# A hybrid attention/mLSTM block: q/k of three mLSTM heads and the branch gates by seven half-size products

## The chip, the cores and the metric

One Trainium2 chip, one core of it. The metric is the device time of one execution in microseconds. The kernel before takes 1360.22 us (median of 3 runs, 1359.88 to 1360.26).

## The reference

One layer on x of 512 tokens and width 1024, float32:

```python
f = swiglu(rmsnorm(x, ffn1_pre_g), w_gate, w_up, w_down)         # d_ff = 2816
x = x + 0.5 * rmsnorm(f, ffn1_post_g)
h = rmsnorm(x, mix_pre_g)
P = h @ w_in        # attention q,k,v | mLSTM q,k | mLSTM v,o | mLSTM i,f | branch gates g_a,g_m
A = dilated_window_attention(...)                  # 4 head slots of 128, 3 groups combined
qk = silu(causal_depthwise_conv(qk_m))             # width 4
M = sigmoid(o) * headnorm(mlstm(q_m, k_m, v_m, i, f))            # 4 heads of 256
y = (sigmoid(g_a) * (A @ w_att) + sigmoid(g_m) * (M @ w_mlstm)) @ w_out
x = x + rmsnorm(y, mix_post_g)
x = x + 0.5 * rmsnorm(swiglu(rmsnorm(x, ffn2_pre_g), ...), ffn2_post_g)
```

## The kernel before

Activations stand transposed in SBUF: `hTh` and `hTl` hold the high and the low part of h (128 partitions, 8 blocks of the width, 512 tokens), and every product with a weight is three matmuls for each of 8 blocks: weight high with h high, weight high with h low, weight low with h high. `load_w` (line 78) brings one weight of 128 x 1024 by a DMA on SyncE's queue into `wf` (3 buffers), casts it on ACT into `wh` and subtracts on DVE into `wl` (5 buffers each; the trace names a buffer after one of its users). `ws` (line 168) does the 24 matmuls of 128 x 512 into one PSUM bank; there are 8 banks.

The stages run one after the other: FFN a (to about 366 us), the attention (to 624), the four mLSTM heads (to 834), the merge (to 965), `w_out` (to 1011), FFN b. Both FFNs make 18 of their units by a form with seven half-size products in place of eight: the operands are cut into quarters (256 tokens, half of the width), sums of quarters of h are made once (`parts`), sums of quarters of the weights for each unit on DVE, and the unit is 7 products of 12 matmuls of 128 x 256 (`seven`, line 278, `product` at line 319). There the order of all engines is written by hand, and DVE's adds read a bank while PE is in the other one.

In the mixer the order on each engine is set by a scheduler when the kernel is built; it can move an instruction of one part between those of another, but each engine then runs its list strictly in order. For a head h: `m_vo(h)` (v and output gate, 96 matmuls), `m_scores`, then the pair of products `m_qk_proj(h + 1, 0)` with its conv `m_qk_conv` (line 874: ACT makes `z`, six DVE ops add the shifted terms, ACT `th`, DVE `z`, ACT cast `mqkh`, DVE `mqkl`), `m_out(h)` (`po`), the pair and conv for `pi` = 1, `m_decay(h + 1)` (`pb`) and `m_turn(h)` (`pml`). The conv reads the pair's two PSUM banks. For the last head the two pairs are those of gates 0 and 1 (`branch_gates`, line 1091). In the merge, for each of 8 `dt`, come 12 matmuls of attention with `wA`, 24 of mLSTM with `wM`, the combination on DVE and ACT, and then the gates' pair of `dt` + 2. The attention's output is kept in SBUF as `atth`, `attl` (lines 861 and 862), and the residual x in four tiles through the whole kernel. The gains of the norms and the small constants come in by POOL's queue, which also computes the norms' powers (`r_pf`, `r_mx`, `r_m`).

Of the kernel before, what the change touches and what calls it, by code (L numbers as in the profile page):

```python
# [39 lines left out]
def tile_hybrid_block(ctx: ExitStack, tc: tile.TileContext, a: dict):  # L40
# [1050 lines left out]
    def branch_gates(dt):
        wg = [load_w(a["wgm"][dt, b], f"gm{dt}{b}") for b in range(2)]
        p1 = pair(f"p1_{dt}")
        for b in range(2):
            ws(p1[b], wg[b], KD, hTh, hTl)
        t1 = work.tile([P, 2, T], F32, tag=("h", "tmp")[dt % 2], bufs=1, name=f"t1_{dt}")
        for b in range(2):
            nc.scalar.activation(t1[:, b, :], p1[b], AF.Tanh, scale=0.5)
# [35 lines left out]
    for dt in range(KD):
        if dt % 2 == 0:
            wA = load_w(a["wA"][dt // 2], f"wA{dt}")
        wM = load_w(a["wM"][dt], f"wM{dt}")
# [2 lines left out]
        ws(p2[0], (wA[0][:, o:o + 512], wA[1][:, o:o + 512]), HEADS, atth, attl)  # L1140
        ws(p2[1], wM, KD, mlTh, mlTl)
        t1 = t1s[dt]
        for b in range(2):
            nc.vector.scalar_tensor_tensor(t1[:, b, :], t1[:, b, :], 1.0, p2[b], op0=ALU.add, op1=ALU.mult)  # L1144
        nc.vector.tensor_tensor(t1[:, 0, :], t1[:, 0, :], t1[:, 1, :], op=ALU.add)
        nc.scalar.mul(meTh[:, dt, :], t1[:, 0, :], 0.5)
        nc.vector.scalar_tensor_tensor(meTl[:, dt, :], t1[:, 0, :], 0.5, meTh[:, dt, :].bitcast(F32),
                                       op0=ALU.mult, op1=ALU.subtract)
# [123 lines left out]
```

## Time and profile before

| | us |
|---|---|
| median of 3 runs | 1360.22 |
| the profiled execution | 1361.59 |
| its span, first to last instruction | 1359.8 |
| PE busy | 1344.6 (99%) |
| PE weight loads (PEld) | 1202.8 (88%) |
| DVE busy | 968.4 (71%) |
| ACT busy | 601.7 (44%) |
| POOL busy | 30.1 (2%) |

The profiled execution is a single one, with 1361.59 us of its own; its span is what the hardware profiler shows from the first instruction to the last. Busy time is the union of an engine's instructions. A matmul's row lasts longer than the distance to the next one, because matmuls are pipelined: the distance from start to start is what one costs. The same holds in a smaller way for DVE and ACT, where an instruction begins a little before the one ahead has ended.

### The profile page before, as it was taken

The numbers are of one execution on the slowest core, as the hardware profiler recorded it, in microseconds if no ns is written. First come the engines' busy times: TensorE is split into PE (matmuls) and PEld (weight loads), VectorE is DVE, ScalarE is ACT, GpSimd is POOL, SyncE is SP. The second block draws the span as 40 slices with busy tenths as digits, with TensorE's granted clock in tenths as the row PEclk, the third lists the DMA queues.
The fourth block names the chain that finished last, engine by engine and source line by source line (L and its number), as shares of the span: only waits on it lengthen the run. The fifth ranks groups of instructions, "written<-read, shape, count | busy, mean of one in ns | idle before, by whom it ended". The sixth has DMA issues, their size and how long they took to land.

```text
span 1359.8 us, 19896 instructions
## 1 busy us (share of the span) xinstructions
PE 1344.6 (99%) x7976; PEld 1202.8 (88%) x7976; DVE 968.4 (71%) x1482; ACT 601.7 (44%) x969; POOL 30.1 (2%) x52
## 2 busy tenths in 40 slices
PE   8999999999999999999999999999999999999998
PEld 7899999878899889888888888888889999998786
DVE  7789898896772885675756754333378798997983
ACT  5444444555633532435545443222264444444552
POOL 1000000000200000000000000000010000000000
PEclk8999999999999999999999999999999999999999
DMA  5333333654233222222222232233213233335541
GB/s 201 94 109 95 109 109 109 232 171 150 69 93 123 78 78 91 81 78 78 78 78 78 78 108 79 95 107 100 95 47 116 94 94 108 109 104 194 174 150 62
DMA packets 40829, 145.91 MB, mean 107 GB/s; under 512 B 4652, under 2 KB 4652, under 8 KB 40736
## 3 DMA queue, kind: packets, MB, share of 16 engines
q1 hardware_dynamic: 39600, 141.08, 31.7%
q0 software_dynamic: 1136, 3.56, 0.8%
q8 instruction: 62, 1.02, 0.3%
q14 instruction: 31, 0.25, 0.1%
HBM read 142.53 MB, written 2.10 MB: 106 GB/s over the span
## 4 chain that ended last, share of the span: by engine, by line
PE 89%; DVE 6%; ACT 2%; issue 2%; DMA 1%; SPq 0%; DVEq 0%; POOLq 0%; ACTq 0%
PE p L176 11%; PE qb_b L319 9%; PE qb_a L319 9%; PE pq L176 8%; PE pm L176 6%; PE qa_b L319 4%; PE qa_a L319 4%; PE acc_o L227 3%; PE pvo L991 2%; PE pvo L993 2%; PE pvo L992 2%; PE pg_a L186 2%; PE pq L186 2%; PE pg_b L186 2%; PE pg_a L176 2%; PE pg_b L176 2%
## 5 line engine op out<-in xcount | busy, mean ns | idle before, releaser
L176 PE MATMUL pq<-hTh_mx,wh_qk 128*128 128x512 f32 x160 | 63.2, 395 | 0.0
L176 PE MATMUL pq<-hTl_mx,wh_qk 128*128 128x512 f32 x160 | 62.4, 390 | 0.0
L88 DVE TENSOR_TENSOR wl_qk<-wf_qk,wh_qk 128x1024 fp32r<-128x1024 f32 x24 | 29.3, 1221 | 41.6 <-ACT wh_qk L86 31.3
L176 PE MATMUL pm<-hTh_mx,wh_mqk 128*128 128x512 f32 x128 | 50.3, 393 | 0.0
L991 PE MATMUL pvo<-wh_vo,hTh_mx 128*128 128x512 f32 x128 | 50.2, 392 | 0.0
L176 PE MATMUL pm<-hTl_mx,wh_mqk 128*128 128x512 f32 x128 | 49.9, 390 | 0.0
L176 PE MATMUL p<-hTh_mx,wh_gm 128*128 128x512 f32 x128 | 49.9, 390 | 0.0
L993 PE MATMUL pvo<-wl_vo,hTh_mx 128*128 128x512 f32 x128 | 49.8, 389 | 0.0
L176 PE MATMUL p<-hTl_mx,wh_gm 128*128 128x512 f32 x128 | 49.8, 389 | 0.0
L992 PE MATMUL pvo<-wh_vo,hTl_mx 128*128 128x512 f32 x128 | 49.8, 389 | 0.0
L86 ACT CAST wh_qk<-wf_qk 128x1024 fp32r<-128x1024 f32 x24 | 25.0, 1045 | 56.1 <-PE pw L739 28.8
L1144 DVE SCALAR_TENSOR_TENSOR t<-t,p 128x512 f32<-128x512 f32 x16 | 11.0, 688 | 42.7 <-PE p L176 42.7
L88 DVE TENSOR_TENSOR wl_mqk<-wf_mqk,wh_mqk 128x1024 fp32r<-128x1024 f32 x16 | 19.6, 1223 | 29.7 <-ACT wh_mqk L86 25.3
L176 PE MATMUL pq<-hTh_mx,wl_qk 128*128 128x512 f32 x160 | 39.6, 389 | 0.0
L882 DVE SCALAR_TENSOR_TENSOR z<-pm,cw,z 128x511 f32<-128x511 f32 (+2 forms) x48 | 35.3, 743 | 1.4 <-ACT z L880 0.9
L319 PE MATMUL qa_a<-hTl_f,wh_a 128*128 128x256 f32 x144 | 36.1, 283 | 0.0
L319 PE MATMUL qa_b<-hTl_f,wh_b 128*128 128x256 f32 x144 | 36.1, 283 | 0.0
L319 PE MATMUL qa_a<-hTh_f,wh_a 128*128 128x256 f32 x144 | 36.1, 283 | 0.0
L319 PE MATMUL qa_b<-hTh_f,wh_b 128*128 128x256 f32 x144 | 36.1, 283 | 0.0
L247 ACT CAST wh_a<-cd_a 128x1024 fp32r<-128x1024 f32 x18 | 18.9, 1050 | 38.9 <-DVE cd_a L247 38.9
L247 ACT CAST wh_b<-cd_b 128x1024 fp32r<-128x1024 f32 x18 | 18.9, 1050 | 37.8 <-DVE cd_b L247 37.8
L176 PEld LDWEIGHTS pq<-hTh_mx,wl_qk 128*128 128x128 f32 x160 | 30.0, 188 | 6.2
(677 smaller groups left out, 4421.1 us busy)
## 6 DMA issues: line engine op xcount, KB each, us to landing
wf_qk<-in_wqk SPq DMA_DIRECT2D x24, 512.0 KB, 3.7
B_a<-in_wdq SPq DMA_DIRECT2D x21, 512.0 KB, 4.1
B_b<-in_wdq SPq DMA_DIRECT2D x21, 512.0 KB, 3.9
g_a<-in_wgu SPq DMA_DIRECT2D x18, 512.0 KB, 3.8
u_a<-in_wgu SPq DMA_DIRECT2D x18, 512.0 KB, 3.8
g_b<-in_wgu SPq DMA_DIRECT2D x18, 512.0 KB, 3.8
u_b<-in_wgu SPq DMA_DIRECT2D x18, 512.0 KB, 3.7
wf_mqk<-in_wmqk SPq DMA_DIRECT2D x16, 512.0 KB, 3.3
```

What stands on the lines that cost most here:

```text
L86: nc.scalar.copy(wh, wf)
L88: nc.vector.tensor_tensor(wl, wf, wh.bitcast(F32), op=ALU.subtract)
L176: nc.tensor.matmul(out, lhsT=wt[:, k * P:(k + 1) * P], rhs=x[:, k, tok], start=n == 0, stop=n == len(terms) - 1)
L186: nc.tensor.matmul(outs[b][:, tok], lhsT=ws_[b][w][:, k * P:(k + 1) * P], rhs=x[:, k, tok], start=i + k + hf == 0, stop=hf == 1 and i == 2 ...
L227: nc.tensor.matmul(out, lhsT=x[:, tk], rhs=w[:, cs], start=first and n == 0, stop=last and n == 2, skip_group_check=True)
L247: self.last[eng] = getattr(getattr(nc, eng), fn)(*args, **kw).ins
L319: nc.tensor.matmul(out, lhsT=wt[:, i * P:(i + 1) * P], rhs=y[:, i, :], start=first and n == 0, stop=last and n == len(terms) - 1, skip_gro ...
L882: nc.vector.scalar_tensor_tensor(z[:, s:], src[:, :T - s], cw[:, ct, 3 - s:4 - s], z[:, s:], op0=ALU.mult, op1=ALU.add)
L991: nc.tensor.matmul(out, lhsT=hTh[:, k, tk], rhs=wh[:, cs], start=k == 0, stop=False)
L992: nc.tensor.matmul(out, lhsT=hTl[:, k, tk], rhs=wh[:, cs], start=False, stop=False)
L993: nc.tensor.matmul(out, lhsT=hTh[:, k, tk], rhs=wl[:, cs], start=False, stop=k == KD - 1)
L1144: nc.vector.scalar_tensor_tensor(t1[:, b, :], t1[:, b, :], 1.0, p2[b], op0=ALU.add, op1=ALU.mult)
```

## The change

It replaces the pair of products of 14 places by a unit of seven half-size products: q and k of mLSTM heads 1 to 3 (two units a head) and the eight gates (one unit for each `dt`, g_a and g_m together). `make_parts`, called between the loads of `m_vo(0)`, makes the four further sums and differences of quarters of h and splits each into high and low. They take the SBUF of x and of the attention's output: x is stored to DRAM by four DMAs on POOL's queue at the end of FFN a, the attention's output (now one float32 tile, without `attl`) by one after the last head slot, and both are loaded again in the merge. The unit collects its four quarters in an SBUF tile `r`, which the conv and the gates read in place of PSUM. The merge becomes: gates 2 to 7, with `wM` of dt 0 to 3 after the first four; reload; `wM` of dt 4 to 7; `wA` and the combination for all dt.

```diff
+    def make_parts(tmp):
...
+        full(t[0], 0, 1)
+        full(t[1], 0, 0)
+        sub_(t[1], t[0], t[1])
+        part(5, t[1])
+        yield
...
+    def unit(n, srcs, r, first_out):
+        g, u = (act.tile([P, 2, Q], F32, tag="wf", bufs=3, name=f"{'gu'[b]}_{n}") for b in range(2))
...
+        take((1, 2), g)
+        take((4,), u[:, 1:2, :])
+        tt(u[:, 1, :], u[:, 0, :], u[:, 1, :], ADD)
+        tt(u[:, 0, :], g[:, 0, :], u[:, 0, :], SUB)
+        tt(g[:, 0, :], u[:, 1, :], g[:, 0, :], SUB)
+        tt(g[:, 1, :], g[:, 1, :], g[:, 0, :], SUB)
+        take((7, 5), u)
+        take((6, 3), g)
+        pa, pb = bank(f"qa_{n}"), bank(f"qb_{n}")
+        qa, qb, qc = pa[:, 0:H], pb[:, 0:H], pb[:, H:T]
...
+        product(qa, 1, True, False)
+        nc.scalar.copy(r[:, 1, 0:H], qa)
+        product(qc, 5, True, False)
+        product(qb, 6, False, False)
+        tt(r[:, :, H:T], pb.rearrange("p (a b) -> p a b", b=H), r[:, 1:2, 0:H].broadcast_to([P, 2, H]), ADD)
+        product(qa, 2, False, True)
+        first_out(r[:, 0, 0:H], qa)
+        product(qb, 7, False, False)
+        tt(r[:, 1, H:T], qb, r[:, 1, H:T], ADD)
+        product(qc, 3, False, False)
+        tt(r[:, 0, H:T], qc, r[:, 0, H:T], ADD)
+        product(qb, 4, False, True)
+        tt(r[:, 1, 0:H], qb, r[:, 1, 0:H], ADD)
...
     def m_qk_proj(h, pi, between=None):
+        if h:
+            r = work.tile([P, 2, T], F32, tag="tmp", bufs=1, name=f"r{h}{pi}")
+            unit(f"mqk{h}{pi}", [a["wmqk"][h, 2 * pi + b] for b in range(2)], r,
+                 lambda out, pa: nc.scalar.copy(out, pa))
+            return r
...
+    def keep_x():
+        for t in range(NT):
+            nc.gpsimd.dma_start(xkeep[t], xs[t])
...
+    attkeep = dram.tile([P, HEADS, T], F32, name="attkeep")
+    nc.gpsimd.dma_start(attkeep, att)
...
+    for dt in range(2, KD):
+        branch_gates(dt, G[dt])
+        if dt - 2 < 4:
+            branch_m(dt - 2)
+    att = hpool.tile([P, KD, T], F32, tag="hTl", name="att2")[:, 0:HEADS, :]
+    nc.gpsimd.dma_start(att, attkeep)
+    atts = new_att("back")
+    for i in range(2):
+        split(att[:, 2 * i:2 * i + 2, :], *(t[:, 2 * i:2 * i + 2, :] for t in atts))
+    xs[:] = new_xs()
+    for t in range(NT):
+        nc.gpsimd.dma_start(xs[t], xkeep[t])
+    for dt in range(4, KD):
+        branch_m(dt)
     for dt in range(KD):
         if dt % 2 == 0:
             wA = load_w(a["wA"][dt // 2], f"wA{dt}")
-        wM = load_w(a["wM"][dt], f"wM{dt}")
-        p2 = pair(f"p2_{dt}")
+        pA = bank(f"p1_{dt}")
...
-        if dt + 2 < KD:
-            branch_gates(dt + 2)
```

How the lists of the engines change shows at three places. First ACT in head 1, around the second pair of q/k of head 2, before (`th`, `mqkh` are those of the first pair's conv, `jm` the norm of `m_out`, `z` reads the pair's banks):

```order
L998 ACTIVATE vml_7106<-ident 128x4x2
L884 ACTIVATE th_6791<-z_6790 128x1024
L1065 ACTIVATE jm_6822,ssm_6807<-po_0_6804,dn_6806 128x256
L1065 ACTIVATE jm_6824,ssm_6807<-po_1_6805,dn_6806 128x256
L1065 ACTIVATE jm_6864,ssm_6837<-po_0_6834,dn_6836 128x256
L887 CAST mqkh_6726<-z_6790 128x1024
L1065 ACTIVATE jm_6866,ssm_6837<-po_1_6835,dn_6836 128x256
L86 CAST wh_vo_7077<-wf_vo_7075 128x1024
L880 ACTIVATE z_6938<-pm_0_6876,cw 128x512
```

and with the change (line 947 is the copy of product 1, line 965 that of product 2; `r_6868` is the first unit's, `r_7070` the second's, and both are one buffer):

```order
L985 ACTIVATE r_6868<-z_6985 128x1024
L988 CAST mqkh_6866<-z_6985 128x1024
L947 COPY r_7070<-qa_mqk_7095 128x256
L1176 ACTIVATE jm_7058,ssm_7031<-po_0_7028,dn_7030 128x256
L1176 ACTIVATE jm_7060,ssm_7031<-po_1_7029,dn_7030 128x256
L86 CAST wh_vo_7265<-wf_vo_7263 128x1024
L965 COPY r_7070<-qa_mqk_7095 128x256
L1130 ACTIVATE E_7205<-gd_7203,cT 128x128
```

The copy of the second unit's product 1, which was not there, stands behind `th` and the cast of the first unit's conv, and a split of `m_vo` comes only after it. On DVE at the same place, with the change (line 986 is the `z` that ACT's cast waits for, line 983 the last of the six conv ops, line 927 the read of products 5 and 6 of the second unit):

```order
L983 SCALAR_TENSOR_TENSOR z_6985<-r_6868,cw,z_6985 128x509
L1182 TENSOR_TENSOR rr_7024<-r_m_7022,dn_7000 128x2
L1171 TENSOR_TENSOR dn_7030<-po_1_7029,cT 128x1
L88 TENSOR_TENSOR wl_vo_7237<-wf_vo_7233,wh_vo_7235 128x1024
L986 SCALAR_TENSOR_TENSOR z_6985<-r_6868,z_6985 128x1024
L1185 SCALAR_TENSOR_TENSOR so_6809<-po_0_6998,rr_7024,so_6809 128x256
L1185 SCALAR_TENSOR_TENSOR so_6809<-po_1_6999,rr_7024,so_6809 128x256
L1172 SCALAR_TENSOR_TENSOR dn_7030<-po_1_7029,dn_7030 128x1
L1173 RECIPROCAL dn_7030<-dn_7030 128x2
L989 TENSOR_TENSOR mqkl_6867<-z_6985,mqkh_6866 128x1024
L927 TENSOR_TENSOR r_7070<-qb_mqk_7096,r_7070 128x2x256
```

Before `z` of the first unit a small norm op and a split of `wl_vo` were let in, and the second unit's first read comes after the conv's last op.

Last PE in the merge, gate 3, from the last matmuls of product 2 (`qa`) over product 7 (the first `qb` rows, on a part) to the start of product 3 (`p_1` is `wM` of dt 1):

```order
L943 MATMUL qa_gm_8467<-hTh_mx,wl_gm_8448 128x256 x4
L943 MATMUL qb_gm_8468<-partsl,wh_gm_8459 128x256 x8
L943 MATMUL qb_gm_8468<-partsl,wl_gm_8460 128x256 x4
L180 MATMUL p_1_8566<-mlm0h_6669,wh_wM_8562 128x512
L180 MATMUL p_1_8566<-mlm0l_6670,wh_wM_8562 128x512
L180 MATMUL p_1_8566<-mlm0h_6669,wh_wM_8562 128x512
L180 MATMUL p_1_8566<-mlm0l_6670,wh_wM_8562 128x512
L943 MATMUL qb_gm_8468<-hTh_mx,wh_gm_8463 128x256
L943 MATMUL qb_gm_8468<-hTl_mx,wh_gm_8463 128x256
```

and PE at a gate's pair before, from the first bank's last matmuls to the second bank's first:

```order
L176 MATMUL p_4_0_8127<-hTl_mx,wh_gm_8117 128x512
L176 MATMUL p_4_0_8127<-hTh_mx,wh_gm_8117 128x512
L176 MATMUL p_4_0_8127<-hTl_mx,wh_gm_8117 128x512
L176 MATMUL p_4_0_8127<-hTh_mx,wl_gm_8119 128x512 x8
L176 MATMUL p_4_1_8128<-hTh_mx,wh_gm_8123 128x512
L176 MATMUL p_4_1_8128<-hTl_mx,wh_gm_8123 128x512
L176 MATMUL p_4_1_8128<-hTh_mx,wh_gm_8123 128x512
```

Where one bank of 24 matmuls followed the other, product 3 now follows product 7 with four `wM` matmuls between them.

## Rows read from the trace of the kernel before

**Rows 1.** The page, parts 1 and 4: busy by engine; the chain by engine.

```profile
PE 1344.6 (99%) x7976; PEld 1202.8 (88%) x7976; DVE 968.4 (71%) x1482; ACT 601.7 (44%) x969; POOL 30.1 (2%) x52
...
PE 89%; DVE 6%; ACT 2%; issue 2%; DMA 1%; SPq 0%; DVEq 0%; POOLq 0%; ACTq 0%
```

**Rows 2.** The chain that ended last: start, us, engine, tile, line, count.

```profile
646.39 3.75 PE pa L1033 x24
...
702.83 10.94 PE pm L176 x48
713.77 3.60 PE po L1056 x30
717.36 10.90 PE pm L176 x48
...
834.50 130.59 PE p L176 x576
```

**Rows 3.** The windows: us, busy us (count) of PE, PEld, DVE, ACT, POOL; clock, DMA share, GB/s.

```profile
1059.00:1233.00 174.00, 174.00 (x1452) 174.00 (x1451) 151.99 (x217) 81.01 (x121) 0.00 (x0) 1.00 0.32 102
260.00:300.00 40.00, 39.18 (x170) 31.37 (x169) 39.41 (x49) 23.71 (x34) 0.00 (x0) 1.00 0.56 190
624.00:699.00 75.00, 75.00 (x355) 62.48 (x354) 48.12 (x78) 37.82 (x71) 1.42 (x2) 1.00 0.24 80
702.00:755.00 53.00, 53.00 (x261) 44.58 (x260) 34.15 (x61) 25.38 (x47) 1.38 (x2) 1.00 0.24 80
834.00:965.00 131.00, 131.00 (x582) 108.52 (x581) 48.74 (x55) 38.01 (x46) 0.00 (x0) 1.00 0.29 97
```

**Rows 4.** The timeline of PE, FFN a: start, us, out<-in, tile, count. Products 1/6, 7/3.

```profile
152.31 0.28 PE L319 MATMUL qb_a<-x6h_a,wh_a 128*128 128x256 f32 x1
...
158.07 0.28 PE L319 MATMUL qb_a<-x7h_a,wh_a 128*128 128x256 f32 x1
158.19 0.28 PE L319 MATMUL qb_a<-x7l_a,wh_a 128*128 128x256 f32 x1
...
159.51 0.28 PE L319 MATMUL qb_a<-hTh_f,wh_a 128*128 128x256 f32 x1
```

**Rows 5.** The timeline of DVE, FFN a, the same unit.

```profile
155.53 0.69 DVE L247 TENSOR_TENSOR uv_a<-qb_a,q_a 128x512 f32<-128x512 f32 x1
156.13 1.22 DVE L247 TENSOR_TENSOR wl_a<-cd_a,wh_a 128x1024 fp32r<-128x1024 f32 x1
157.27 0.42 DVE L247 TENSOR_TENSOR z_a<-qb_a,q_a 128x256 f32<-128x256 f32 x1
...
161.15 0.76 DVE L247 TENSOR_TENSOR z_a<-qb_a,uv_a 128x256 f32<-128x256 f32 x2
```

**Rows 6.** The timeline of ACT, FFN a, the same unit.

```profile
152.51 0.37 ACT L247 COPY q_a<-qa_a 128x256 f32<-128x256 f32 x1 [0.23 <-PE qa_a L319]
155.05 1.05 ACT L247 CAST wh_a<-cd_a 128x1024 fp32r<-128x1024 f32 x1 [2.16 <-DVE cd_a L247]
```

**Rows 7.** The timelines of DVE and PE in heads.

```profile
624.45 0.69 DVE L1015 TENSOR_TENSOR gd<-pb,caus 128x512 f32<-128x512 f32 x1 [2.73 <-PE pb L1013]
...
627.75 4.04 DVE L882 SCALAR_TENSOR_TENSOR z<-pm,cw,z 128x511 f32<-128x511 f32 x6 [0.88 <-ACT z L880]
...
728.20 0.49 PE L1012 MATMUL pb<-selr 4*128 4x512 f32 x1
...
728.85 1.09 PE L1083 MATMUL pml<-ident,so 128*128 128x128 f32 x8
```

**Rows 8.** The timelines of POOL and ACT at the end of FFN a.

```profile
345.59 0.55 POOL L100 TENSOR_TENSOR r_mx<-v_mx,nhalf 128x1 f32<-128x1 f32 x1 [2.87 <-DVE v_mx L111]
...
366.26 1.05 ACT L86 CAST wh_qk<-wf_qk 128x1024 fp32r<-128x1024 f32 x1 [1.27 <-DMA wf_qk<-in_wqk]
```

**Rows 9.** The page, part 6: DMA issues, KB each, us to landing.

```profile
out<-x SPq DMA_DIRECT2D x8, 256.0 KB, 2.0
...
g_f1post<-in_ffn_post_g POOLq DMA_DIRECT2D x1, 512.0 KB, 5.1
```

More of the change, by code (lines that the diff above doesn't have):

```diff
@@ L112, in mean_rsqrt, with new_xs @@
         return rsqrt(v, 1, name)
-    xs = [const.tile([P, D], F32, name=f"x{t}") for t in range(NT)]
+    def new_xs():
+        return [const.tile([P, D], F32, tag=f"x{t}", bufs=1, name=f"x{t}") for t in range(NT)]
+    xs = new_xs()
+    dram = ctx.enter_context(tc.tile_pool(name="dram", bufs=1, space=bass.MemoryType.DRAM))
     def scratch(name, *where):
@@ L687, in tile_hybrid_block, with new_att @@
     low = mctx.enter_context(tc.tile_pool(name="low", bufs=1))
-    atth = low.tile([P, HEADS, T], F32R, name="atth")
-    attl = low.tile([P, HEADS, T], F32R, name="attl")
+    def new_att(name):
+        return [low.tile([P, HEADS, T], F32R, tag=f"att{x}", bufs=1, name=f"{name}{x}") for x in "hl"]
+    att = low.tile([P, HEADS, T], F32, tag="atth", bufs=1, name="att")
     cw = mix.tile([P, 16, 5], F32, name="cw")
@@ L860, in values, with quad, part @@
                                  start=False, stop=j == 3 and g == 1, skip_group_check=True)
-        nc.scalar.copy(atth[:, h, :], o)
-        nc.vector.tensor_tensor(attl[:, h, :], o, atth[:, h, :].bitcast(F32), op=ALU.subtract)
-    def m_qk_proj(h, pi, between=None):
+        nc.scalar.copy(att[:, h, :], o)
+    x7 = {}
+    def make_parts(tmp):
+        def quad(t, i, j):
+            return t[:, 4 * i:4 * i + 4, j * H:(j + 1) * H]
+        x7.update({k: (quad(hTh, i, j), quad(hTl, i, j)) for k, (i, j) in {1: (0, 0), 2: (1, 0), 3: (1, 1)}.items()})
+        t = [v[:, 0:4 * H].rearrange("p (a b) -> p a b", b=H) for v in tmp]
+        full = lambda out, i, j: nc.vector.tensor_tensor(out, quad(hTh, i, j).bitcast(F32), quad(hTl, i, j).bitcast(F32),
+                                                         op=ADD)
+        sub_ = lambda out, p, q: nc.vector.tensor_tensor(out, p, q, op=SUB)
+        places = {4: (const, ("x0", "x1")), 5: (const, ("x2", "x3"))}
+        rest = {6: 0, 7: 1}
+        deep = new_att("parts")
+        def part(k, src):
+            if k in places:
+                pool, tags = places[k]
+                h, l = (pool.tile([P, 4, H], F32R, tag=g, bufs=1, name=f"p{k}{y}") for g, y in zip(tags, "hl"))
+            else:
+                h, l = (deep[rest[k]].rearrange("p a b -> p (a b)")[:, y * 4 * H:(y + 1) * 4 * H]
+                        .rearrange("p (a b) -> p a b", b=H) for y in range(2))
+            split(src, h, l)
+            x7[k] = (h, l)
+        full(t[0], 0, 1)
[3 more added lines that the diff above has]
+        yield
+        full(t[2], 1, 1)
+        sub_(t[1], t[2], t[1])
+        part(6, t[1])
+        yield
+        sub_(t[0], t[2], t[0])
+        part(7, t[0])
+        yield
+        full(t[2], 1, 0)
+        sub_(t[1], t[2], t[1])
+        part(4, t[1])
+        yield
@@ new lines, in unit, with take, product @@
+    def unit(n, srcs, r, first_out):
+        g, u = (act.tile([P, 2, Q], F32, tag="wf", bufs=3, name=f"{'gu'[b]}_{n}") for b in range(2))
+        for t, src in zip((g, u), srcs):
+            nc.sync.dma_start(t, src.rearrange("p (q c) -> p q c", c=Q))
+        w = {}
+        def take(keys, src):
+            m = len(keys)
+            wh, wl = (wpool.tile([P, WMAX], F32R, tag=f"w{y}", bufs=5, name=f"w{y}{keys[0]}_{n}")[:, :m * Q]
+                      .rearrange("p (q c) -> p q c", c=Q) for y in "hl")
+            split(src, wh, wl)
+            for i, k in enumerate(keys):
+                w[k] = (wh[:, i, :], wl[:, i, :])
+        tt = lambda out, p, q, op: nc.vector.tensor_tensor(out, p, q, op=op)
+        take((1, 2), g)
[8 more added lines that the diff above has]
+        qa, qb, qc = pa[:, 0:H], pb[:, 0:H], pb[:, H:T]
+        def product(out, k, first, last):
+            (wh, wl), (xh, xl) = w[k], x7[k]
+            terms = [(wh, y, i) for i in range(4) for y in (xh, xl)] + [(wl, xh, i) for i in range(4)]
+            for m, (wt, y, i) in enumerate(terms):
+                nc.tensor.matmul(out, lhsT=wt[:, i * P:(i + 1) * P], rhs=y[:, i, :], start=first and m == 0,
+                                 stop=last and m == len(terms) - 1, skip_group_check=True)
+        product(qa, 1, True, False)
[11 more added lines that the diff above has]
+        tt(r[:, 1, 0:H], qb, r[:, 1, 0:H], ADD)
@@ L979, in tile_hybrid_block, with m_vo @@
         m_qk_conv(0, pi, pqs[pi], qk)
-    def m_vo(h):
+    def m_vo(h, between=iter(())):
         pv = [bank(f"pvo{h}{j}") for j in range(NT)]
@@ L993, in m_vo @@
                     nc.tensor.matmul(out, lhsT=hTh[:, k, tk], rhs=wl[:, cs], start=False, stop=k == KD - 1)
+            next(between, None)
         vm = [lp.tile([P, NT, MDH + 2], F32R, tag=f"vm{x}", bufs=1, name=f"vm{x}{h}") for x in "hl"]
@@ L1089, in tile_hybrid_block, with branch_gates, early_gates @@
     t1s = {}
[L1091 to L1098, printed above, removed]
-        t1s[dt] = t1
+    def branch_gates(dt, t1):
+        t1s[dt] = t1
+        unit(f"gm{dt}", [a["wgm"][dt, b] for b in range(2)], t1,
+             lambda out, pa: nc.scalar.activation(out, pa, AF.Tanh, scale=0.5))
+        rest = t1.rearrange("p a b -> p (a b)")[:, H:]
+        nc.scalar.activation(rest, rest, AF.Tanh, scale=0.5)
+    def early_gates(dt):
+        branch_gates(dt, work.tile([P, 2, T], F32, tag=("h", "tmp")[dt], bufs=1, name=f"t1_{dt}"))
     E = m_decay(0)
     for h in range(MH):
-        vm, so = m_vo(h)
+        tmp = [] if h else [lp.tile([P, n], F32, tag=g, bufs=1, name=f"pt_{g}") for g, n in (("vmh", 1032), ("vml", 1032), ("so", 1024))]
+        vm, so = m_vo(h, iter(()) if h else make_parts(tmp))
         EE = m_scores(h, qk, E)
@@ L1121, in tile_hybrid_block @@
     mg = gctx.enter_context(tc.tile_pool(name="merge", bufs=1))
-    meTh = mg.tile([P, KD, T], F32R, name="meTh")
-    meTl = mg.tile([P, KD, T], F32R, name="meTl")
+    G = [mg.tile([P, 2, T], F32, tag=f"G{dt}", bufs=1, name=f"G{dt}") for dt in range(KD)]
+    me = []
     class Tiles:
@@ L1136, in tile_hybrid_block @@
             wA = load_w(a["wA"][dt // 2], f"wA{dt}")
-        wM = load_w(a["wM"][dt], f"wM{dt}")
-        p2 = pair(f"p2_{dt}")
+        pA = bank(f"p1_{dt}")
         o = (dt % 2) * 512
[L1140 to L1148, printed above, removed]
-        if dt + 2 < KD:
-            branch_gates(dt + 2)
+        ws(pA, (wA[0][:, o:o + 512], wA[1][:, o:o + 512]), HEADS, *atts)
+        s0, s1 = G[dt][:, 0, :], G[dt][:, 1, :]
+        nc.vector.scalar_tensor_tensor(s0, t1s[dt][:, 0, :], 1.0, pA, op0=ADD, op1=MUL)
+        v = work.tile([P, D], F32, tag="gain", bufs=2, name=f"me_{dt}")[:, :T]
+        nc.vector.tensor_tensor(v, s0, s1, op=ADD)
+        me.append(mg.tile([P, 2, T], F32R, tag=f"G{dt}", bufs=1, name=f"meT{dt}"))
+        nc.scalar.mul(me[dt][:, 0, :], v, 0.5)
+        nc.vector.scalar_tensor_tensor(me[dt][:, 1, :], v, 0.5, me[dt][:, 0, :].bitcast(F32), op0=MUL, op1=SUB)
     g_mpost = gain(a["mix_post_g"], "mpost")
```

19 lines of the change are left out of this document (13 added, 6 removed).

## The prediction

> **What bounds the kernel now.** The page comes first: PE is busy 99% of the span, and it holds 89% of the chain that ended last, DVE 6%, ACT 2% [rows 1]. So only PE time that goes counts, and only where nothing else takes the gap. The chain, read at the stages that the diff touches, then shows PE without a break: in a head, one pair of products (10.94 us), the 30 `po` products (3.60), another pair (10.90), and in the merge 576 full matmuls in one piece of 130.59 [rows 2]. The windows show what stands beside it: in 702 to 755 PE is busy all 53.00 us, DVE 34.15, ACT 25.38; in 834 to 965 DVE has 48.74 of 131.00. The granted clock is 1.00 (2.4 GHz) in all of them [rows 3]. DVE is therefore far from a bound here, but the change gives it much work.
>
> **What goes from PE.** A pair is 48 matmuls of 128x512 in 10.92 us on average: 0.2275 from start to start [rows 2]. The seven products are 84 of 128x256. Their price is in the trace, since both FFNs use the same form: a matmul starts every 0.120 us, so a product of 12 takes 1.44 [rows 4], a unit 10.08. Gain 0.84 a unit. There are 14 units, 6 for q/k of heads 1 to 3 and 8 gates: **-11.8 us** (-5.0 in the heads, -6.7 in the gates). The 960 other matmuls of the merge and `po`, `pvo`, `pml` stay.
>
> The Trainium skill ("TensorE: Matmul & The Clock Gate", Back-to-back issue gap) puts the gap of a warm matmul at N/2.4 + 2.5 ns, that is 109.2 and 215.8 ns for 256 and 512 columns; PE's part by it would be -1.19 a unit and -16.6 in all, by the rows -11.8. This case's trace disagrees (120 and 227.5), and the measurement decides.
>
> **What DVE and ACT get.** Start to start on DVE a split of 1024 takes 1.14, a sum of 512 0.60, a 256 read of PSUM about 0.35 [rows 5]. A pair has two splits, 2.28. A unit has three splits of 1024 (3.42), one of 512 (0.60), four sums (2.40), one 512 read (0.60) and three of 256 (1.05): 8.07, so +5.8. `make_parts` adds 12 ops of 1024, 13.7 us, once, in `m_vo(0)`; `attl` goes (0.60 a head). All of this lies beside PE work; it costs what PE waits for, and only the dependences tell that. I walked the new order with these durations, with casts of 1.05 and copies of 0.37 on ACT, and with 0.20 from PE's last matmul to the start behind it (product 6 starts at 152.31 [rows 4], the copy of product 1 at 152.51 [rows 6]). The waits:
>
> - **Entry.** From some 623.9, where the attention's tiles come free (DVE now starts again at 624.45), 15 ops of 1024, five of 512 and six conv ops of 0.66 [rows 7] stand ahead of head 0's first `E` on DVE: 17.1 + 3.0 + 4.0 = 24.1, to 648.0, with ACT waits 648.3. `pa`'s first third is there at about 647.9 [rows 2]: 0.3.
> - **Head 0 to 1.** Behind `E` DVE has no slack: 48.12 us of old work in 624 to 699 [rows 3], plus 13.7 and 11.6, is 73.4 in the 73.3 that remain. The walk gives 0.7 at product 5's low half, 0.8 and 0.8 at products 5 and 6 of the second unit, 2.0 at its product 2: 4.3. Bounds: at the DVE share of the stretch where DVE is fullest beside an almost unbroken PE, 39.41 of 40.00 [rows 3], it would be 1.2; at that of the FFN's units, 151.99 of 174.00, 10.7. The walk lies between, and I take it.
> - **Heads 1 to 2 and 2 to 3.** The new rows of ACT show the place: `COPY r` of the second unit stands behind the cast `mqkh` of the first one's conv, because `r` has one buffer. After product 4 of the first unit: 0.2, add 0.35, six conv ops 3.96, small ones 0.4, then a `wl_vo` split over `th` 1.35, `zz` 1.14, cast 1.05, copy 0.37, 0.1 of handing over: 8.9. PE has till then 16 `po` (1.92), three products (4.32), two `pb` 0.65 and four of eight `pml` 0.5 [rows 7], a `pvo` 0.23: 7.6. Wait 1.3. Another 0.6 falls between products 7 and 3 of the first unit. 1.9 a head, twice: 3.8. Bounds: 0 (conv first on DVE) and 3 (all small ops late).
> - **Gates.** In steady state (dt 2 to 5) product 3 waits for the add after product 7, and that stands on DVE behind the next unit's first split; its `wh` is the slot that product 2 frees (five slots, five casts a turn). From product 2's end: 0.2 + 1.05 + 1.14 + 0.42 = 2.8; PE has product 7 and four `wM` matmuls, 1.44 + 0.91 = 2.35. Wait 0.5, four times, 2.1 with a late load; dt 0 and 1 together 1.1, dt 6 and 7 0.8 (no `wM` between).
>
> The Trainium skill ("PSUM — Partial Sum Buffer", PSUM bank collisions raise a hardware error) says to guard PSUM by bank, not by address, and this speaks against the unit, whose products 7, 3 and 4 share one bank and are read between. If two halves could be used apart, the waits between 7, 3 and 4 would go, about 4 us, and the sum would be -3. The trace fits the rule: the FFN goes from product 7 to 3 with no gap [rows 4], and reads both halves only later, by two ops of 256 at 161.15 [rows 5], when PE is in the other bank.
>
> **Moved transfers.** Storing x: four DMAs on POOL's queue, each ahead of an `r_mx` before which POOL idles 2.87, so an issue fits. The last store runs beside a `wf_qk` that ACT already waits 1.27 for [rows 8]: 0 to 1 us, taken as 0. Storing att: issued at the end of `values(3)`, some 624, and its slot is written again by the cast of part 6, by the walk at 640; 256 KB out took 2.0 us and 512 KB in 5.1 [rows 9], so 1 MB is 8 to 10: 0 to 1, taken as 0. Reloading att: issued when product 3 of the last gate has read `hTl`, needed after four `wM` rows of 24, 21.8 us. Two transfers of 512 KB at 5.1 and the two splits (1.14 + 1.05 each) are 14.6: hidden, 7 to spare. x and the gains follow on that queue with a stage of 46 us before the first use: hidden. In the `wA` stage DVE has 2.5 of 2.73 a dt: fits, 0 to 1.
>
> **Sum.** 0.3 + 4.3 + 3.8 + 4.0 = 12.4 of waits against 11.8: **+0.6**. The profiled execution took 1361.59 (span 1359.8), 1.4 above the median 1360.22; laid on the median, **1360.9**. That is inside the 0.2% (2.7 us, 1357.5 to 1362.9) that a measurement of this kernel can tell from no change.
>
> **Rivals.**
> - *The side work hides.* DVE keeps ahead, as in 260 to 300 where 98.5% of DVE cost PE 0.8 in 40 us [rows 3]. Waits of 0 to 8 us: 1348.4 to 1356.6; likeliest 1354. For it: DVE idles 19 us of 702 to 755, and PE's list has `po`, `pvo` or `wM` rows between most products. Against: the FFN's form, at 87% of DVE without a wait, has an order in which an add always stands under another product, and `unit` has not. Chance 0.29.
> - *Slower: DVE becomes the bound in the heads.* Place: the second unit's product 2, and all of head 0 to 1. Price: 10.7 for head 0 to 1 as above, 3 for each of the other two, 4.5 for the gates: 20.5, so 1360.2 - 11.8 + 20.5 = 1368.9; half of the excess gives 1365. It decides from the point where DVE in 624 to 699 can't pass 95% or so, since every further per cent costs 0.8 us. For it: in-order DVE with waits on ACT and PE in every unit. Against: 100% is close in 260 to 300. Chance 0.28.
> - *The reload of att comes late.* POOL holds two x loads ahead of it; if these take turns with it, 20 us pass instead of 10, and 0 to 4 us are lost: 1361 to 1365. Chance 0.04.
> - *The change doesn't shorten PE.* With three bank changes a unit, half-size matmuls could start every 0.130, and 84 x 0.130 is again 10.92: 1360.2 + 12.4 = 1372.6. The FFN shows 0.120 with the same form [rows 4]. Chance 0.02.
> - *Half the columns in half the time*: at half of 0.2275, 0.114, a unit takes 9.56, 1.36 less than a pair, 19.1 in all: 1360.2 - 19.1 + 12.4 = 1353.5. The 0.120 of the rows speaks against it; chance 0.01. The gap that the Trainium skill ("TensorE: Matmul & The Clock Gate", Back-to-back issue gap) states would come near it, at -16.6 in place of -19.1.
>
> **How the numbers follow.** Forecast case 0.36. Faster: 0.29 + 0.01 = 0.30. Slower: 0.28 + 0.02, 0.02 of the reload and 0.01 of the forecast's upper edge, 0.33; the same 0.37. Range 1353 to 1368: it leaves out the lower part of the first rival (0.09), the upper end of the second (0.07) and the fourth. The likeliest case's own range is 1357.5 to 1363.
>
> **What would show it.** In the profile after: units at 84 x 0.120; PE busy about 12 less and its idle time 12 more; DVE busy about 1060 (968.4 + 13.7 + 14 x 5.8 - 2.4). Idle time before `qa_mqk` with the releaser ACT `r`, of 1 to 2 us in heads 1 and 2; before `qb_gm` with the releaser DVE, 0.5 each; the largest loss between 650 and 700. Wrong: DVE under 90% in 624 to 699 with no PE gap (first rival), `p1` waiting for DMA (third), or waits before a `qa` of gates that I have as hidden.

## The result, and the profile after

The changed kernel takes 1364.08 us (median of 7 runs, 1362.84 to 1365.29); the kernel before, run beside it, 1359.88 (7 runs, 1359.68 to 1360.26). The ratio is 1.0031 [1.0019, 1.0042], so it is slower by 4.2 us. The forecast was 1360.9, within 0.2% of before. The time lies in the range of 1353 to 1368, but beyond the 1357.5 to 1363 of that case.

| us | before | after |
|---|---|---|
| the profiled execution, its span | 1361.59, 1359.8 | 1365.29, 1363.5 |
| to the first `pa` (attention scores of head 0) | 646.23 | 644.31 |
| head 0 to 1, 1 to 2, 2 to 3 (`pa` to `pa`) | 52.68, 52.68, 52.68 | 56.65, 54.93, 54.97 |
| head 3 with gates 0, 1, and the merge (`pa` to `w_out`) | 160.66 | 157.66 |
| `w_out` to FFN b | 45.36 | 45.37 |

With 0.84 less for each unit and nothing else, a head would take 51.00 and the last long stage 153.94. So 5.65, 3.93, 3.97 and 3.72 were lost: 17.3 of waits, late starts and matmuls at a lower clock against 11.8 gained. The 1.9 us that the first 646 us lack are no part of the change. They come from the first microseconds of FFN a, where the granted clock was 0.93 on average up to 24 us in this execution and 0.86 in that of before; from there to the first `pa` the distance between the two stays at 2.0 to 1.9.

Page 1 of after answers to [rows 1]:

```profile
PE 1341.8 (98%) x8480; PEld 1219.6 (89%) x8480; DVE 1061.1 (78%) x1632; ACT 635.3 (47%) x1023; POOL 37.4 (3%) x62
```

DVE has the 1060 that were expected. PE's busy time fell by 2.8, not by 12, and its idle time rose by 6.5 (span less busy, 15.2 to 21.7). A row that starts late behind a matmul not yet ended, or that runs at a lower clock, counts as busy.

The windows of after, as [rows 3]:

```profile
624.00:699.00 75.00, 71.40 (x411) 61.41 (x410) 69.77 (x109) 42.77 (x77) 2.62 (x2) 1.00 0.24 77
699.00:752.00 53.00, 51.24 (x321) 46.33 (x320) 43.62 (x78) 28.80 (x51) 1.81 (x2) 0.97 0.25 79
752.00:804.00 52.00, 50.24 (x316) 45.47 (x316) 43.98 (x79) 28.68 (x53) 1.47 (x2) 0.97 0.22 72
834.00:965.00 131.00, 130.04 (x825) 116.85 (x825) 88.32 (x118) 53.37 (x68) 2.68 (x5) 1.00 0.40 133
```

DVE is full only in the first (93%); the two heads behind it lose nearly 4 us each with DVE at 82 and 85%, and there the clock is no longer 1.00. PE's waits, by what they waited for (us in total, times, longest):

```profile
PE pml L1194 <- DVE so L1185: 3.8, 3, 1.8
...
PE qb_mqk L943 <- DVE r L927: 1.4, 2, 1.2
...
PE qb_gm L943 <- DVE G L927: 1.0, 2, 0.8
PE qb_mqk L943 <- DVE wl_mqk L243: 0.9, 2, 0.5
PE pvo L1103 <- DVE wl_vo L88: 0.8, 1, 0.8
```

The longest is one that the forecast did not have: `pml`, the turning of `so` in `m_turn`. The timeline of after around it in head 1, first PE:

```profile
723.41 0.39 PE L1124 MATMUL pb<-Gl,selr 4*128 4x512 f32 x1
725.57 0.83 PE L1194 MATMUL pml<-ident,so 128*128 128x128 f32 x4 [1.76 <-DVE so L1185]
726.16 0.48 PE L1101 MATMUL pvo<-wh_vo,hTh_mx 128*128 128x512 f32 x1
726.52 0.39 PE L943 MATMUL qa_mqk<-hTh_mx,wh_mqk 128*128 128x256 f32 x1
...
727.41 0.42 PE L943 MATMUL qa_mqk<-hTl_mx,wh_mqk 128*128 128x256 f32 x1
727.62 0.41 PE L943 MATMUL qa_mqk<-hTh_mx,wh_mqk 128*128 128x256 f32 x1
```

then DVE and ACT:

```profile
717.41 0.41 DVE L927 TENSOR_TENSOR r<-qb_mqk,r 128x256 f32<-128x256 f32 x1
...
722.77 1.22 DVE L88 TENSOR_TENSOR wl_vo<-wf_vo,wh_vo 128x1024 fp32r<-128x1024 f32 x1
723.90 1.22 DVE L986 SCALAR_TENSOR_TENSOR z<-r,z 128x1024 f32<-128x1024 f32 x1
725.04 0.87 DVE L1185 SCALAR_TENSOR_TENSOR so<-po,rr,so 128x256 f32<-128x256 f32 x2
```

```profile
725.15 1.05 ACT L988 CAST mqkh<-z 128x1024 fp32r<-128x1024 f32 x1 [2.02 <-DVE z L986]
726.10 0.37 ACT L947 COPY r<-qa_mqk 128x256 f32<-128x256 f32 x1
```

The first `so` stands on DVE behind the conv, a split and `z`, so PE stops for 1.76 at `pml`. What was forecast for product 2 is there too: the copy of product 1 that it waits for runs from 726.10 to 726.47, its first matmul follows at 726.52. And behind the standstill the matmuls of product 2 start 0.21 apart in place of 0.12. The windows say why (the number after POOL's is the granted clock):

```profile
722.00:724.00 2.00, 1.81 (x12) 1.23 (x10) 1.42 (x5) 1.06 (x1) 0.59 (x1) 1.00 0.00 0
724.00:726.00 2.00, 0.43 (x3) 0.24 (x3) 1.97 (x4) 0.85 (x1) 0.00 (x0) 1.00 0.43 111
726.00:728.00 2.00, 2.00 (x12) 1.80 (x12) 1.93 (x4) 1.50 (x6) 0.00 (x0) 0.74 0.38 152
728.00:730.00 2.00, 2.00 (x11) 1.90 (x10) 1.52 (x5) 1.71 (x4) 0.69 (x1) 0.50 0.00 0
730.00:732.00 2.00, 2.00 (x14) 1.88 (x14) 1.80 (x4) 2.00 (x7) 0.00 (x0) 0.90 0.22 33
```

Some four microseconds hold a stretch at 0.50 (1.2 in place of 2.4 GHz), with PE "busy" all the while.

### The profile page after: what moved, and what is told of

It reads as the page before. It is cut to its first block, busy times and chain, and to the rows that moved or that the text cites. A ratio compares the mean times of both kernels' runs of the same rounds, so it can differ in the third digit from the quotient of the medians.

```text
span 1363.5 us, 21149 instructions
## 1 busy us (share of the span) xinstructions
PE 1341.8 (98%) x8480; PEld 1219.6 (89%) x8480; DVE 1061.1 (78%) x1632; ACT 635.3 (47%) x1023; POOL 37.4 (3%) x62
## 5 line engine op out<-in xcount | busy, mean ns | idle before, releaser
L231 PE MATMUL acc_o<-wh_od,meT 128*128 128x512 f32 x128 | 39.6, 391 | 0.0
L180 PEld LDWEIGHTS pq<-hTh_mx,wh_qk 128*128 128x128 f32 x160 | 30.1, 188 | 6.1
L180 PEld LDWEIGHTS pq<-hTl_mx,wh_qk 128*128 128x128 f32 x160 | 30.1, 188 | 6.0
L251 DVE TENSOR_TENSOR wl_a<-ab_a,wh_a 128x1024 fp32r<-128x1024 f32 x18 | 22.0, 1224 | 14.1 <-ACT wh_a L251 14.1
L251 DVE TENSOR_TENSOR wl_b<-ab_b,wh_b 128x1024 fp32r<-128x1024 f32 x18 | 22.0, 1224 | 14.1 <-ACT wh_b L251 14.1
L1103 PEld LDWEIGHTS pvo<-wl_vo,hTh_mx 128*128 128x128 f32 x128 | 24.1, 188 | 6.0 <-DVE wl_vo L88 1.3
L1101 PEld LDWEIGHTS pvo<-wh_vo,hTh_mx 128*128 128x128 f32 x128 | 24.1, 188 | 4.8 <-issue 0.4
```

Source lines behind the costliest of these rows:

```text
L180: nc.tensor.matmul(out, lhsT=wt[:, k * P:(k + 1) * P], rhs=x[:, k, tok], start=n == 0, stop=n == len(terms) - 1)
L231: nc.tensor.matmul(out, lhsT=x[:, tk], rhs=w[:, cs], start=first and n == 0, stop=last and n == 2, skip_group_check=True)
L251: self.last[eng] = getattr(getattr(nc, eng), fn)(*args, **kw).ins
```

## The experiments

Two explanations stood against each other. By the first, the loss is **order**: in each head one standstill at `pml`, the low clock behind it, and the parts in head 0. By the second, DVE has too much **work**, and what is freed at one place is lost at the next. "Heads" below are the three distances `pa` to `pa`, "merge" is the stage from the last `pa` to `w_out`; medians are given with the ratio to the kernel before on the same chip (1359.76 for the first four runs, 1360.17 for the next four, 1360.21 for three, 1359.78 for the last).

**1. Only the gates.** q and k of heads 1 to 3 go back to pairs.

```diff
     def m_qk_proj(h, pi, between=None):
-        if h:
-            r = work.tile([P, 2, T], F32, tag="tmp", bufs=1, name=f"r{h}{pi}")
-            unit(f"mqk{h}{pi}", [a["wmqk"][h, 2 * pi + b] for b in range(2)], r,
-                 lambda out, pa: nc.scalar.copy(out, pa))
-            return r
...
```

> q/k of heads 1-3 again by pairs of full products; gates, parts, DRAM and merge order as changed. Theory A (the loss lies in the heads: in changed minus before, from the first pa to the last pa +8.5 us, merge -3.0): the heads go back to 52.7 a head, the merge keeps -3.0, so 1357 (1356 to 1358.5). Rival B (DVE is too full once the parts are made, whatever the heads do): head 0 keeps 1 to 3 us of waits, 1358.5 to 1360. Rival C (the merge and the moved tensors cost the time): 1362 or more.

Measured: 1356.72, 0.9978 [0.9970, 0.9987]; heads 52.68 each, merge 157.82.

**2. Only the heads.** The gates go back to pairs.

```diff
-        unit(f"gm{dt}", [a["wgm"][dt, b] for b in range(2)], t1,
-             lambda out, pa: nc.scalar.activation(out, pa, AF.Tanh, scale=0.5))
...
+        wg = [load_w(a["wgm"][dt, b], f"gm{dt}{b}") for b in range(2)]
+        p1 = pair(f"pg{dt}")
+        for b in range(2):
+            ws(p1[b], wg[b], KD, hTh, hTl)
...
```

> Gates again by pairs of full products, in the changed merge order; heads by seven products. Theory A: the heads keep +8.5, the merge loses its -3.0, so 1368 (1366.5 to 1369.5). Rival B: the same. Rival C (the gates' units are what costs): 1358 to 1361.

Measured: 1367.13, 1.0054 [1.0042, 1.0067]; heads 56.31, 54.96, 54.29, merge 160.66. The halves add up: the gates gain 3.0, the heads lose 7.4, together 4.3 slower, against 4.2 for both. The reordered merge and the reload of att cost nothing with pairs. The reload of x is not tried by it: with the gates in pairs x's tiles come free sooner, and it is issued at 776 to 791, in head 2 to 3.

**3. `m_turn` later.** It is put behind the first quarter of the next head's `m_vo`, so that `pml` no longer stands right behind `pb`.

```diff
+    def late_turn(h, so):
+        m_turn(h, so)
+        yield
...
-        vm, so = m_vo(h, iter(()) if h else make_parts(tmp))
+        vm, so = m_vo(h, late_turn(h - 1, so) if h else make_parts(tmp))
...
-        m_turn(h, so)
+    m_turn(MH - 1, so)
```

> m_turn(h) of heads 0 to 2 is placed after the first quarter of m_vo(h+1), so PE has up to 24 pvo matmuls (5.5 us) to do while so is still being made. Theory A (PE's wait of 1.76 us for so in heads 1 and 2, and the half clock that follows it, make 3.7 us a head): both go, at most 1.3 a head come back at product 2: 1357 to 1360, clock 1.00 in both heads. Rival B (DVE's load is the bound, the wait only shows where PE happens to need DVE): the wait moves to pvo or to product 2 and the time stays within 1 us of 1364.

Measured: 1358.33, 0.9989 [0.9980, 0.9999] (one of its 11 executions took 2196.89, at a mean granted clock of 0.556; no run shows why); heads 56.66, 51.92, 51.93, merge 156.71. The same stretch in its windows:

```profile
722.00:734.00 12.00, 11.71 (x71) 9.80 (x70) 10.25 (x20) 9.04 (x19) 1.12 (x2) 1.00 0.26 87
```

No operation was taken from DVE, and 3.0 us a head came back: order, not work. Nothing became ready sooner either. The copy of product 1 ends 25.52 after head 1's `pa`, in after 25.51, and product 2 starts at 25.71 in place of 25.56. But till then PE has done ten `pvo` matmuls, where in after it did one and four `pml`:

```profile
723.58 0.50 PE L1101 MATMUL pvo<-wh_vo,hTh_mx 128*128 128x512 f32 x1
...
726.28 0.39 PE L1101 MATMUL pvo<-wh_vo,hTh_mx 128*128 128x512 f32 x1
726.51 0.28 PE L943 MATMUL qa_mqk<-hTh_mx,wh_mqk 128*128 128x256 f32 x1
```

Head 0 to 1 was not helped: its wait at `pml`, 0.32 in after, went, but one of 1.12 behind `pb` was followed by a lower clock (0.58 and 0.57 in 668 to 672), which that head does not have in after. The merge is 0.95 shorter, without the two waits that after has there.

**4. Eight more matmuls ahead of `pb`** in heads 2 and 3, their output overwritten. They fill the standstill and leave all else in place; if the clock is a cost of its own, that part comes back.

```diff
         gbc = bank(f"pb{h}")
+        for i in range(8 if h > 1 else 0):
+            nc.tensor.matmul(gbc, lhsT=hTh[:, i % KD, 0:P], rhs=hTh[:, i % KD, :], start=True, stop=True)
```

> 8 additional matmuls of 128x512 (1.82 us) ahead of pb in heads 1 and 2, whose output is overwritten: PE works where it waited 1.76 us; so does not come earlier. Theory A2 (the clock falls to 1.2 GHz because PE has stood still): pml starts when it did, within 0.2, the clock stays at 1.00, 1.5 to 2 us a head come back: 1360 to 1361. Rival (the clock falls by itself there, or PE's wait is not tied to so): no gain, 1364, or 1367.7 if the 3.6 us simply add.

Measured: 1361.97, 1.0015 [1.0006, 1.0024]; heads 56.05, 53.65, 53.69, merge 156.88. Its timeline of PE, and its windows:

```profile
722.64 2.00 PE L1124 MATMUL pb<-hTh_mx 128*128 128x512 f32 x8
...
725.24 0.83 PE L1196 MATMUL pml<-ident,so 128*128 128x128 f32 x4
...
726.53 0.28 PE L943 MATMUL qa_mqk<-hTh_mx,wh_mqk 128*128 128x256 f32 x1
726.65 0.28 PE L943 MATMUL qa_mqk<-hTl_mx,wh_mqk 128*128 128x256 f32 x1
```

```profile
722.00:734.00 12.00, 12.00 (x75) 9.87 (x74) 10.47 (x20) 9.71 (x21) 0.94 (x2) 1.00 0.27 87
```

`pml` starts as late as in after, but product 2 has its 0.12 again and the clock is 1.00: 1.28 us a head for work that computes nothing. What was expected here was 1.5 to 2.

**5. Both 256 reads after product 3**, on top of run 3, in all units.

```diff
         product(qb, 7, False, False)
-        tt(r[:, 1, H:T], qb, r[:, 1, H:T], ADD)
         product(qc, 3, False, False)
+        tt(r[:, 1, H:T], qb, r[:, 1, H:T], ADD)
         tt(r[:, 0, H:T], qc, r[:, 0, H:T], ADD)
```

> As e3_turn_late (1358.3), and in every unit both 256 reads after product 3, so that product 3 follows product 7 with no read between. Theory A (the read between 7 and 3 holds product 3 by 0.2 to 0.5 a unit, in gates and heads): 14 x 0.25 = 3.5 less, of which the later wait of product 4 for two reads takes up to 2: 1355.5 to 1357.5. Rival (PE's filler rows already hide both reads): 1358, same.

Measured: 1359.68, 0.9996 [0.9988, 1.0005]; heads 57.70, 51.52, 51.53, merge 157.76. A miss: 0.4 is gained in each of the two later heads, but PE now stops at product 4, which waits for both reads (1.70 and 1.69), and in head 0 to 1 also 2.54 at a `pvo`, for ACT's cast of its weight.

```profile
PE pvo L1101 <- ACT wh_vo L86: 2.5, 1, 2.5
...
PE qb_mqk L943 <- DVE r L927: 1.7, 1, 1.7
PE qb_gm L943 <- DVE G L927: 1.7, 1, 1.7
```

The first two are in head 0 to 1, the third in gate 7.

**6. Without the parts.** `make_parts` makes no sums (products 4 to 7 use quarters of h in their place, so the output lacks those sums); all else as in after.

```diff
...
-        part(5, t[1])
...
+        x7.update({k: x7[{4: 2, 5: 1, 6: 3, 7: 1}[k]] for k in (4, 5, 6, 7)})
...
```

> The changed kernel without the four sums of quarters of h and their splits (12 DVE ops and 4 casts less; quarters of h stand in their place, so the units compute something else). Theory A (head 0 to 1, 56.65 where 51.0 would be had, loses its 5.6 us to the 13.7 us of parts on DVE): that head falls to 52 to 53, the heads behind stay at 54.9, total 1360 (1359 to 1361). Rival (the units' own splits, sums and the conv chain make it): head 0 to 1 falls only to the 54.9 of the others: 1362 to 1363.

Measured: 1362.19, 1.0015 [1.0006, 1.0024]; heads 54.87, 54.91, 54.68, merge 156.39. The rival held: without the 13.7 us of work on DVE head 0 to 1 gets back only 1.8 of its 5.65, and stops at `pml` like the others.

```profile
PE pml L1165 <- DVE so L1156: 5.3, 3, 1.8
```

This 1.8 is the price of the parts in the order of after, and not a fixed one. With `m_turn` late (run 3) the other heads take 51.92 and head 0 to 1 still 56.66, so there up to 4.7 hang on the parts; no run has both edits. Without the parts x also comes back at once, in FFN a, so that no load of x stands beside the last gate.

**7. Head 1 by pairs**, on top of run 3 (the parts then lie beside PE work that asks little of DVE).

```diff
-        if h:
+        if h > 1:
             r = work.tile([P, 2, T], F32, tag="tmp", bufs=1, name=f"r{h}{pi}")
```

> As e3_turn_late (1358.3), with q/k of head 1 again by pairs, so that the parts have the whole of head 0 to be made in and only heads 2 and 3 use them. Theory A: head 0 to 1 goes from 56.65 to 52.68, the others stay at 51.9: 1354.3 (1353.5 to 1355.5). Rival (parts cost their time wherever they are): head 0 to 1 at 54 or more, 1356 to 1358.

Measured: 1354.28, 0.9956 [0.9942, 0.9969]; heads 52.72, 51.92, 51.92, merge 156.75. Faster than both kernels.

**8. Runs 5 and 7 together.**

> e10 and e8 together. Theory A: 1352 to 1354; rival of e8: the same as e10.

Measured: 1355.60, 0.9967 [0.9955, 0.9980]; heads 52.72, 51.51, 51.54, merge 157.92. A miss: the heads gain their 0.4 each, and the merge gives 1.2 back, at product 4 of gate 7 (1.86 in one wait).

**9. Run 8 with the late reads in the heads alone** (`if n[0] != "g"` around the moved line).

> e10 (1354.3), with both 256 reads behind product 3 in the units of heads 2 and 3 alone, not in the gates, where one product 4 waited 1.9 us in e11. Theory A (a read between 7 and 3 costs about 0.2 a unit even where the profile shows no idle time): those two heads at 51.5 instead of 51.9, the merge as in e10 (156.75): 1353.5 (1352.8 to 1354.2). Rival (e11's 51.5 was chance of the schedule): as e10, 1354.3.

Measured: 1354.27, 0.9957 [0.9944, 0.9971]; heads 52.73, 51.52, 51.48, merge 156.47. The stages are as expected; the 0.8 do not show in the median, which equals run 7's.

**10. Run 7 with the second of head 1's pairs as a unit** (`2 * h + pi > 2` in place of `h > 1`).

> As e10, but the second of head 1's two pairs by seven products too, so the parts have half of head 0 to be made in. Theory (parts cost only where units follow them at once): head 0 to 1 at 51.9 to 52.7, total 1353.5 to 1354.3. Rival (DVE is too full in head 0 for any unit): head 0 to 1 at 53.5 or more: 1355 to 1357.

Measured: 1354.77, 0.9962 [0.9950, 0.9975]; heads 52.31, 51.92, 51.92, merge 158.68. The head gives its 0.4; the merge loses 1.9, in one wait of 2.03 at gate 7, although nothing was changed there.

**11. Runs 9 and 10 together.**

> e12 and e13 together: by the theories 1352.8 to 1353.6; by their rivals 1355 to 1357.

Measured: 1353.27, 0.9953 [0.9940, 0.9965]; heads 52.06, 51.52, 51.48, merge 156.92.

**12. Run 8 with x loaded later.** Gate 7's wait came and went with edits elsewhere, so its cause was sought in what runs beside it: x, 2 MB, is reloaded on POOL's queue when the products of gate 7 set its tiles free. Here a memset on DVE holds each load until the combination of `dt` 1.

```diff
...
+    xs[:] = new_xs()
+    for t in range(NT):
+        with tc.issue_after(last[1]):
+            nc.vector.memset(xs[t][:, 0:1], 0.0)
+        nc.gpsimd.dma_start(xs[t], xkeep[t])
```

> As e11 (1355.6), but x comes back from DRAM only after wA of dt 1 (a small memset of each x tile on DVE holds the DMA). Theory D (product 4 of gate 7 waits 1.86 in e11 because DVE's read stands behind a wM split whose load lands late beside the reload of x): that wait falls under 0.4, the merge from 157.9 to 156.3, total 1353.8 to 1354.2. Rival (the load is late because its buffer comes free late, with or without x): wait and time as in e11, 1355.6.

Measured: 1353.12, 0.9952 [0.9938, 0.9965]; heads 52.73, 51.47, 51.55, merge 156.24. The timelines of ACT and POOL at gate 7, run 8:

```profile
908.29 1.05 ACT L86 CAST wh_wM<-wf_wM 128x1024 fp32r<-128x1024 f32 x1 [2.31 <-PE qa_gm L943]
...
911.79 1.05 ACT L86 CAST wh_wM<-wf_wM 128x1024 fp32r<-128x1024 f32 x1 [2.16 <-DMA wf_wM<-in_wM]
```

```profile
905.64 1.24 POOL L1268 DMA_DIRECT2D x<-xkeep  x2 [83.09 <-PE qb_gm L943]
```

and run 12:

```profile
907.94 1.05 ACT L86 CAST wh_wM<-wf_wM 128x1024 fp32r<-128x1024 f32 x1 [2.32 <-PE qa_gm L943]
...
909.63 1.05 ACT L86 CAST wh_wM<-wf_wM 128x1024 fp32r<-128x1024 f32 x1 [0.36 <-DMA wf_wM<-in_wM]
```

```profile
941.59 2.09 POOL L1286 DMA_DIRECT2D x<-xkeep  x4 [29.96 <-DVE x L1285]
```

Without the two loads of x beside it, the weight of `wM` is there 1.8 us sooner, its split leaves DVE sooner, and the read that product 4 waits for with it; the wait of 1.86 is gone. The merge is where it was expected, the time 0.7 below the expected range. Runs 11 and 12 are the fastest, 6.9 and 6.7 us below the kernel before, and not to be told apart.

## Why the prediction came out as it did

- **What goes from PE** held. In gate 7 of after, products 6 and 2 show it: 1.43 from the first matmul of one to that of the next, as in [rows 4].

```profile
916.56 1.11 PE L943 MATMUL qb_gm<-partsh,wh_gm 128*128 128x256 f32 x8
917.51 0.64 PE L943 MATMUL qb_gm<-partsh,wl_gm 128*128 128x256 f32 x4
917.99 0.28 PE L943 MATMUL qa_gm<-hTh_mx,wh_gm 128*128 128x256 f32 x1
```

  The rivals of 0.130 and 0.114 fall. The 109.2 ns that the formula of the Trainium skill gives for 256 columns ("TensorE: Matmul & The Clock Gate", Back-to-back issue gap) are not reached here either.
- **Entry, 0.3**, was nothing: the first `pvo` of head 0 starts at 622.42 (624.34 before), and `pa` follows 21.89 later in both.

```profile
622.42 0.50 PE L1101 MATMUL pvo<-wh_vo,hTh_mx 128*128 128x512 f32 x1
```

- **Heads 1 to 2 and 2 to 3, 1.9 a head, is the step that failed**: 3.95 were lost. The walk was right that the conv and the copy of product 1 hold product 2: in after its first matmul follows that copy by 0.05. But the way from the end of product 4 of the first unit to product 2 took 9.8 (716.76 to 726.52) where the walk had 8.9. DVE begins the add 0.65 after product 4 and not 0.2, behind two splits of weights, and it idles 0.58 for a norm's power of POOL, for which the walk had no term:

```profile
722.62 0.16 DVE L1182 TENSOR_TENSOR rr<-r_m,dn 128x2 f32<-128x2 f32 x1 [0.58 <-POOL r_m L100]
```

  The walk also counted the four `pml` ahead of product 2 as work that PE does meanwhile [rows 7]; they need `so`, and that too stands on DVE behind `z`. So PE stood at `pml`, for 1.76 in one piece, and the sign named for this place, idle time before `qa_mqk` with the releaser ACT `r`, is nowhere in the list of after. And the sum had no term for the clock: 1.28 a head by run 4. Wait and clock make 3.04; run 3 gives back 3.01 (54.93 to 51.92). The remaining 0.9 are small late starts, of which run 9 recovers 0.4.
- **Head 0 to 1, 4.3**, was too small by 1.35, and its reason only partly right. The profile shows six waits there, 3.45 in all, the longest 1.15 at product 3, and none at product 2 of the second unit, where the walk had 2.0. Run 6 prices the parts at 1.8 in this order; without them the head loses what the other heads lose. "Behind `E` DVE has no slack" fits the 93% of the windows; yet taking the parts away leaves 3.9 of 5.65. How the 5.65 divide is not shown further than that.
- **Gates, 4.0**, held in sum (3.72) and only partly in kind, so that the sum is in part luck. Product 3 is held by a read that stands on DVE behind other work (in gate 7 behind a split, as forecast), but by about 0.2 a gate and not 0.5. The list has only 1.0 of waits, 0.75 of it at product 4 of gate 7. Most of the rest is starts about 0.2 late behind a read of DVE, 0.1 ahead of the first matmul and 0.1 behind it, that show as no idle time:

```profile
921.57 0.40 PE L180 MATMUL p<-mlm0l,wh_wM 128*128 128x512 f32 x1
921.89 0.39 PE L943 MATMUL qb_gm<-hTh_mx,wh_gm 128*128 128x256 f32 x1
922.11 0.28 PE L943 MATMUL qb_gm<-hTl_mx,wh_gm 128*128 128x256 f32 x1
```

  0.32 and 0.22 from start to start, for rows that elsewhere take 0.23 and 0.12. The read that product 3 waits for ends at 921.83, 0.06 ahead of it:

```profile
921.41 0.42 DVE L927 TENSOR_TENSOR G<-qb_gm,G 128x256 f32<-128x256 f32 x1
```

- **Moved transfers** as hidden: true of the stores, since up to the first `pa` no more than 0.1 is lost, and of att, by run 2, where the merge with its reload is 160.66 as before. Not of x: with units, two of its four loads are issued beside the last gate, and by run 12 they delay a load of `wM` there. Only run 12 takes them away and leaves the rest of the kernel, but the traces agree. From issue to landing that load takes 4.2 and 4.3 with no x beside it (runs 12 and 6), 5.0 to 5.6 with x in runs 3, 4, 7 and 9, where product 4 of gate 7 does not wait, and 5.8 to 7.6 in after and in runs 1, 5, 8, 10 and 11, where it waits 0.28 to 2.03. So in these traces the load is slower beside x each time, and whether it comes too late differs from kernel to kernel; what makes it 5.0 or 7.6 is not shown. The forecast knew that two of the four loads go ahead of att and asked whether they delay att (its third rival: no wait for `wA` or att is listed, so it falls); what else is loaded then, it did not ask.
- **The rivals.** "DVE becomes the bound in the heads" gave 1365 to 1368.9, near the time, but by a mechanism that run 3 refutes for two heads of three: the same work on DVE, placed otherwise, costs 3.0 less a head. That the measured time lies in the range is thus owed to a rival's price and not to the walk. (That price is also added up wrongly: 10.7, 3, 3 and 4.5 make 21.2 and not 20.5, so 1369.6; and the upper end of the first rival is 1356.4, not 1356.6.) "The side work hides" is what run 7 comes close to (1354.28 against 1354), but only with `m_turn` moved and head 1 taken back to pairs.
- **The sum**: 12.4 of waits forecast, 17.3 measured by stages; the difference is 4.1 in the two later heads and 1.35 in head 0 to 1, less 0.3 each in the entry and the gates. In the profiled execution the start hides 1.9 of it: 17.3 - 11.8 - 1.9 = 3.6, and the spans differ by 3.7. That the medians differ by 4.2 is within the spread of the runs.

Left open: whether a second buffer for `r` would free the copy of product 1. It was not tried.

## What to carry to other kernels

When work is moved to an engine with slack, walk every instruction of the bound engine between the last known start and the next, small ones too, and ask for each behind what its operand now stands on the other engine's list; the first that is late sets the stop. A stop of some two microseconds may cost more than itself, through the clock, so first try to place other independent work of the same engine there. And a "hidden" transfer is only hidden if nothing that shares its time is waited for.
